# Retention of 1024 tokens in two halves: pairs of tokens within a half, a split sum of keys by decayed values for the other half

## The chip, the cores and the metric

The kernel runs on one core of a Trainium2 chip. The metric is the time of one execution on the device in microseconds (us); lower is better. The core has five engines that run side by side, each in the order of its own list of instructions: TensorE (PE in the profile, its weight loads PEld), VectorE (DVE), ScalarE (ACT), GpSimd (POOL) and SyncE (SP). SP issues nearly all transfers here, one after the other, so a transfer that waits holds back those that stand behind it.

## What is computed

One encoder layer for two sequences, a sample of 1024 tokens and a prompt of 512. The change touches one part of it, the retention mixer, which works on four heads of 128 features. The reference goes through each sequence in chunks of 128 tokens with a running state, once forward and once backward. Cut to what matters:

```
q = rotary(heads(u[..., :D_RET]))
k = rotary(heads(u[..., D_RET:2 * D_RET])) * (RET_HEAD_DIM ** -0.5)
v = heads(u[..., 2 * D_RET:3 * D_RET])
...
s = einsum('bhncd,bhnjd->bhncj', qc, kc) * Dm        # pairs within a chunk, decayed
intra = einsum('bhncj,bhnje->bhnce', s, vc)
...
Rn = R * gC + einsum('bhcd,bhce->bhde', kk, vv)      # state: keys by decayed values
cross = einsum('bhncd,nbhde->bhnce', qc * wq, states)
return (intra + cross).reshape(B, H, L, d)
...
o = o_f + o_b
o = o * lax.rsqrt(mean(o * o, axis=-1, keepdims=True) + NORM_EPS)
return jax.nn.silu(g) * o
```

Written out, the output of token c is the sum over all tokens j of (q_c . k_j) times decay(|c - j|) times v_j, with one decay rate forward and one backward. The decay is an exponential, so for tokens j that all lie on one side of c it splits into a factor of c and a factor of j.

## The kernel before

All matrix products are made from 32-bit operands split into a high and a low part (`hi_act`, line 59, on ACT makes the high part; `lo`, line 62, the low one), and `mm3` (lines 67 to 69) adds three products of them in PSUM.

The part in question is the third stage of the layer's middle. On PE it holds two kinds of work, interleaved. The main work projects the prompt's 512 tokens with `w_in` (tile `wips`, 24 blocks of 24 products each; function `w_in_pass`) and makes their values (tile `v`, 96 products; function `w_in_v`). Beside it runs `retention`, first for the sample (four heads of 1024 tokens), then for the prompt (512 tokens). `gen_run(main, side, per)` writes both into the program: after each step of the main work, `per` steps of the side work. The build then orders each engine's list with a scheduler that goes by its own estimate of times, so what stands where on an engine is not the written order.

`retention` for one head of 1024 tokens loads q, k and v of all tokens (tile `qkraw`, `vraw`) and splits them (`qkh`, `qkl`, `vh`, `vl`; the low parts on POOL). Then, for each half of 512 tokens and each of the eight blocks of 128 keys: three products give the scores (`st`), DVE multiplies them with the decay (`sm`, line 999), ACT and DVE split the result (`sh`, `sl`), and three products add it to the output (`o`). These are 16 such pairs for a head, 6 products of 512 columns each. The decay of a head (`mask`, function `decay`) is a table over the distance of two tokens, 1920 columns wide. Behind each half comes a tail that normalises it: two products (`ss`), a row of ACT (`row`), and then, through SP and POOL in turn, `cmp`, `rs`, `rr` and `y`.

The program goes on with `load_mats` (tile `mraw`, then `mh` and `ml`: matrices that the next stage needs) and `filter_spectra` (tile `ftap`, transposed into `tr` on PE, then `fw`). The matrices are loaded into the memory of the activations that the projections read, so they can't start before the last `wips` product.

The stage ahead of it (function `mix_in_consts`, `ret_consts`, then `w_in_pass` for the sample beside the filter's own work `filter_taps`, tile `tapps`) starts with loads of constants, among them `delta`, the distances for `decay`.

Of the kernel before, what the change touches and what calls it, by code (L numbers as in the profile page):

```python
# [8 lines left out]
F32 = mybir.dt.float32  # L9
# [37 lines left out]
class Kern:  # L47
# [885 lines left out]

    def ret_consts(self, p):
        nc = self.nc
        self.delta = p.tile([128, 1920], F32, name="delta", bufs=1)
        nc.sync.dma_start(self.delta, self.io["delta"])
        self.lg = p.tile([128, 2, 4], F32, name="lg", bufs=1)
        for i, n in enumerate(("lgf", "lgb")):
            nc.sync.dma_start(self.lg[:, i], self.io[n].broadcast_to([128, 4]))  # L940
        self.nlb = p.tile([128, 4], F32, name="nlb", bufs=1)
        nc.vector.tensor_scalar(self.nlb, self.lg[:, 1], -1.0, None, ALU.mult)
        self.lscale = p.tile([128, 1], F32, name="lscale", bufs=1)
        nc.gpsimd.memset(self.lscale, float(np.log(128.0 ** -0.5)))

    def decay(self, p, h, a, b):


        nc = self.nc
        arg = p.tile([128, 1920], F32, tag="mask", name="mask", bufs=2)  # L950
        lf, lb, nlb = self.lg[:, 0, h:h + 1], self.lg[:, 1, h:h + 1], self.nlb[:, h:h + 1]
        c = slice(896, 1024)
# [4 lines left out]
        nc.scalar.activation(arg[:, a:896], self.delta[:, a:896], AF.Exp, bias=self.lscale, scale=nlb)  # L957
        nc.scalar.activation(arg[:, c], arg[:, c], AF.Exp, bias=self.lscale)
        nc.scalar.activation(arg[:, 1024:b], self.delta[:, 1024:b], AF.Exp, bias=self.lscale, scale=lf)
        return arg  # L960

    def retention(self, L, base, h, d, p, pss, pso):
        nc = self.nc
        nj = L // 128
        cols = slice(base, base + L)
        arg = self.decay(p, h, 896 - (L - 128), 896 + L)
        hn = 1024 // L
        if h % hn == 0:
            qk = []
            for i in range(2):  # L970
                raw = p.tile([128, hn, L], F32, tag="qkraw", name="qkraw", bufs=2)
                for j in range(hn):
                    nc.sync.dma_start(raw[:, j], d["qk"][4 * i + h + j][:, cols])
                hi = p.tile([128, hn, L], F32R, tag=f"qkh{i}", name="qkh", bufs=2)
                lo = p.tile([128, hn, L], F32R, tag=f"qkl{i}", name="qkl", bufs=2)
                self.hi_act(hi, raw)
                self.lo(nc.gpsimd, lo, raw, hi)
                qk += [hi, lo]
            raw = p.tile([128, nj, hn * 128], F32, tag="qkraw", name="vraw", bufs=2)
            for j in range(nj):  # L980
                nc.sync.dma_start(raw[:, j], d["v"][base // 128 + j][:, h * 128:(h + hn) * 128])
            hi = p.tile([128, nj, hn * 128], F32R, tag="vh", name="vh", bufs=2)
            lo = p.tile([128, nj, hn * 128], F32R, tag="vl", name="vl", bufs=2)
            self.hi_act(hi, raw)
            self.lo(nc.gpsimd, lo, raw, hi)
            self.qkv = qk + [hi, lo]
        qh, ql, kh, kl = (t[:, h % hn] for t in self.qkv[:4])
        vh, vl = (t[:, :, h % hn * 128:h % hn * 128 + 128] for t in self.qkv[4:])
        yield
        for c0 in range(0, L, 512):  # L990
            cc = slice(c0, c0 + 512)
            o = pso.tile([128, 512], F32, tag="o", name="o")
            for j in range(nj):
                s = pss.tile([128, 512], F32, tag="st", name="st")
                jj = slice(j * 128, j * 128 + 128)
                self.mm3(s, kh[:, jj], kl[:, jj], qh[:, cc], ql[:, cc], True, True)
                x = c0 - 128 * j + 896
                sm = p.tile([128, 512], F32, tag="sm", name="sm", bufs=4)
                nc.vector.tensor_tensor(sm, s, arg[:, x:x + 512], ALU.mult)
                sh = p.tile([128, 512], F32R, tag="sh", name="sh", bufs=4)  # L1000
                sl = p.tile([128, 512], F32R, tag="sl", name="sl", bufs=4)
                self.hi_act(sh, sm)
                self.lo(nc.vector, sl, sm, sh)
                self.mm3(o, vh[:, j], vl[:, j], sh, sl, j == 0, j == nj - 1)
                if j % 2:
                    yield
            sq = p.tile([128, 512], F32, tag="sq", name="sq", bufs=1)
            nc.scalar.activation(sq, o, AF.Square)
            sh = p.tile([128, 512], F32R, tag="sqh", name="sqh", bufs=1)
            sl = p.tile([128, 512], F32R, tag="sql", name="sql", bufs=1)  # L1010
# [41 lines left out]
    def build(self, xs, outs):  # L1052
# [22 lines left out]
        with ExitStack() as right:  # L1075
# [10 lines left out]
            with pool("raw", 2) as raw, pool("w", 4) as wp, pool("scw") as gp, pool("rope") as rop:  # L1086
                self.mix_in_consts(gp, rop)
                self.ret_consts(rop)
                with pool("g", 4) as gp, pool("nrm") as self.np, pool("xin", 2) as self.xp, pool("hT2") as hp2, pool("wi", 2, space=PSUM) as psw, \
# [122 lines left out]
def dft_consts():  # L1212
# [10 lines left out]
    for L in (1024,512):  # L1223
# [7 lines left out]
    c['delta']=(np.arange(1920)[None]-896-np.arange(128)[:,None]).astype(np.float32)  # L1231
    return c


# [15 lines left out]
```

## Time and profile before

| | before |
|---|---|
| median of 3 runs | 3393.17 us (3390.63 to 3396.44) |
| profiled execution: time, span of the profile | 3399.09 us, 3397.3 us |
| PE busy, share of the span | 3087.7 us, 91% |
| DVE busy | 2644.2 us, 78% |
| ACT busy | 1431.3 us, 42% |
| POOL busy | 555.3 us, 16% |
| first `st` product, last `y` of the retention's tails | 1493.6 us, 1786.0 us |
| last `wips` product of the stage | 1800.2 us |

Busy time is the time in which an engine had an instruction at work; for a PE that is fed without a gap it is 100% of a stretch. The times of the trace count from the start of the span.

### The profile page before, as it was taken

The page shows a single profiled execution, that of the slowest core. Times are in us where ns is not written, and L with a number is a line of the kernel's source. Part 1 is how long each engine was busy: PE and PEld are TensorE (multiplying, and loading weights), DVE is VectorE, ACT ScalarE, POOL GpSimd, SP SyncE. Part 2 cuts the span into 40 slices and gives each one's busy share as a digit, 9 for nine tenths or more (in the row PEclk, how much of TensorE's full clock was granted, in tenths as well). Part 3 has the DMA queues.
Part 4 walks back from the last instruction along what each step waited for, and adds up shares of the span by engine and source line. Part 5 has one row for each costly group of instructions (what it writes and reads, how often), then busy time and mean ns, then how long its engine had stood idle before and what let it go on. Part 6 is the DMA issues. An engine that isn't in the chain of part 4 may idle for free. (4 is left out here: it accounts for less than half of the span.)

```text
span 3397.3 us, 46267 instructions
## 1 busy us (share of the span) xinstructions
PE 3087.7 (91%) x16792; PEld 2885.7 (85%) x16792; DVE 2644.2 (78%) x4316; ACT 1431.3 (42%) x2373; POOL 555.3 (16%) x400
## 2 busy tenths in 40 slices
PE   5999998999897799989897998984899999999996
PEld 4999998999897677767676887763899999999996
DVE  8788788777877599678655878886888788877776
ACT  4333464333444234355543344332433455333453
POOL 0000000000200323365322544552000000000000
PEclk8999999999998899999998999997999999999998
DMA  3567454322344534453453125454377544422343
GB/s 128 211 232 286 123 156 143 84 72 75 103 131 139 169 117 160 150 172 112 120 173 128 44 83 172 153 172 139 127 266 272 190 147 134 143 72 72 87 128 131
DMA packets 218806, 485.34 MB, mean 143 GB/s; under 512 B 36432, under 2 KB 64464, under 8 KB 216400
## 3 DMA queue, kind: packets, MB, share of 16 engines
q1 hardware_dynamic: 218576, 482.37, 43.3%
q8 instruction: 132, 2.16, 0.3%
q14 instruction: 98, 0.80, 0.1%
HBM read 382.60 MB, written 99.65 MB: 142 GB/s over the span
## 5 line engine op out<-in xcount | busy, mean ns | idle before, releaser
L68 PE MATMUL dn<-xl,w2h 128*128 128x384 f32 x1232 | 414.8, 337 | 12.7 <-DVE xl L62 12.7
L59 ACT ACTIVATE wh<-raw 128x512 fp32r<-128x512 f32 (+1 forms) x312 | 216.6, 694 | 446.0 <-PE ua L68 96.4
L59 ACT ACTIVATE wh<-s 128x512 fp32r<-128x512 f32 x352 | 221.7, 631 | 427.7 <-PE ua L68 122.3
L69 PE MATMUL dn<-xh,w2l 128*128 128x384 f32 x1232 | 392.4, 337 | 0.0
L67 PE MATMUL dn<-xh,w2h 128*128 128x384 f32 x1232 | 386.8, 337 | 1.7 <-ACT xh L59 1.6
L59 ACT ACTIVATE w2h<-raw 128x512 fp32r<-128x512 f32 (+1 forms) x348 | 236.6, 682 | 342.4 <-PE dn L68 214.9
L62 DVE TENSOR_TENSOR wl<-s,wh 128x512 fp32r<-128x512 f32 x352 | 241.8, 688 | 168.5 <-PE ub L68 84.2
L95 POOL TENSOR_TENSOR r<-m,mhalf 128x3 f32<-128x3 f32 (+1 forms) x35 | 38.8, 1108 | 1847.8 <-DVE m L94 1846.9
L62 DVE TENSOR_TENSOR w2l<-raw,w2h 128x512 fp32r<-128x512 f32 (+1 forms) x316 | 219.5, 705 | 126.0 <-ACT w2h L59 107.7
L67 PE MATMUL wips<-hh,wh 128*128 128x512 f32 x576 | 231.9, 403 | 17.7 <-ACT wh L59 16.7
L68 PEld LDWEIGHTS dn<-xl,w2h 128*128 128x128 f32 x1232 | 232.5, 189 | 15.3 <-DVE xl L62 15.3
L67 PEld LDWEIGHTS dn<-xh,w2h 128*128 128x128 f32 x1232 | 229.5, 189 | 3.8 <-ACT xh L59 3.3
L69 PE MATMUL wips<-hh,wl 128*128 128x512 f32 x576 | 230.7, 401 | 1.8 <-POOL wl L62 1.2
L68 PE MATMUL wips<-hl,wh 128*128 128x512 f32 x576 | 230.8, 401 | 0.0
L69 PEld LDWEIGHTS dn<-xh,w2l 128*128 128x128 f32 x1232 | 230.5, 189 | 0.0
L62 DVE TENSOR_TENSOR wl<-raw,wh 128x512 fp32r<-128x512 f32 (+1 forms) x276 | 199.0, 721 | 39.9 <-ACT wh L59 37.9
L67 PE MATMUL fw<-th,mh 128*128 128x256 f32 x448 | 132.3, 297 | 30.9 <-DVE spec L839 18.2
L67 PEld LDWEIGHTS wips<-hh,wh 128*128 128x128 f32 x576 | 110.4, 192 | 46.3 <-ACT wh L59 17.6
L67 PE MATMUL ua<-b11h,wh 128*128 128x384 f32 x352 | 123.7, 351 | 26.6 <-ACT b11h L59 26.6
L69 PEld LDWEIGHTS wips<-hh,wl 128*128 128x128 f32 x576 | 110.3, 192 | 30.0 <-POOL wl L62 2.4
L68 PE MATMUL fw<-tl,mh 128*128 128x256 f32 x448 | 132.3, 296 | 1.3 <-DVE tl L62 1.2
L69 PE MATMUL fw<-th,ml 128*128 128x256 f32 x448 | 130.1, 291 | 3.8 <-POOL ml L62 3.0
(342 smaller groups left out, 9088.9 us busy)
## 6 DMA issues: line engine op xcount, KB each, us to landing
raw<-ffn_w SPq DMA_DIRECT2D x440, 256.0 KB, 2.7
raw<-ws SPq DMA_DIRECT2D x220, 256.0 KB, 2.6
wsum<-ffn_w SPq DMA_DIRECT2D x60, 768.0 KB, 7.5
raw<-w_in_f SPq DMA_DIRECT2D x48, 512.0 KB, 4.3
ws<-wsum SPq DMA_DIRECT2D x30, 768.0 KB, 4.2
xq<-x SPq DMA_DIRECT2D x16, 768.0 KB, 7.2
res<-x SPq DMA_DIRECT2D x16, 768.0 KB, 6.3
raw<-w_out SPq DMA_DIRECT2D x24, 512.0 KB, 3.4
```

The lines of the kernel that those rows point to most:

```text
L59: self.nc.scalar.activation(hi, src, AF.Copy)
L62: eng.tensor_tensor(lo, src, hi.bitcast(F32), ALU.subtract)
L67: mm(ps, lhsT=ah, rhs=bh, start=first, stop=False, **kw)
L68: mm(ps, lhsT=ah, rhs=bl, start=False, stop=False, **kw)
L69: mm(ps, lhsT=al, rhs=bh, start=False, stop=last, **kw)
L95: nc.gpsimd.tensor_tensor(r, m, self.mhalf[:, :n], ALU.pow)
```

## The change

For the sample, `retention` now goes through the pairs of tokens of one half only: 8 pairs of 512 tokens with 128 keys for a head in place of 16. What the other half adds to a half's output comes from a new function, `half_state`. It transposes k of the other half on PE (`kt`, four of 128 columns) and splits it (`kth`, `ktl`), multiplies v with its part of the decay (`vs`, four of ACT) and splits it (`vsh`, `vsl`), and sums keys by values over the four blocks (`rs`, 12 products of 128 columns). The sum is split (`rsh`, `rsl`), q is multiplied with its part of the decay (`qw`) and split (`qsh`, `qsl`), and three products add the result to `o` (line L67 to L69, `o<-qsh,rsh` and so on) ahead of the pairs. For a head this happens twice, once for each half. The decay's table shrinks from 1920 columns to 896. `ret_consts` loads a table of distances (`dist`) and one of positions (`kdist`), and ACT makes the factors of the keys (`kw`, 8 small exponentials) there. Buffers change: three for `qkraw` and `vraw` in place of two, three for `sm`, `sh` and `sl` in place of four, shared with the tail. Two steps of the side work follow each step of the main work in place of four. The prompt's retention (512 tokens, one half) keeps its pairs.

The diff, without what only repeats:

```
     def ret_consts(self, p):
         nc = self.nc
-        self.delta = p.tile([128, 1920], F32, name="delta", bufs=1)
+        self.delta = p.tile([128, 896], F32, name="delta", bufs=1)
         nc.sync.dma_start(self.delta, self.io["delta"])
+        self.dist = p.tile([128, 2, 512], F32, name="dist", bufs=1)
+        nc.sync.dma_start(self.dist, self.io["dist"].broadcast_to([128, 2, 512]))
+        kd = p.tile([128, 2, 4], F32, name="kdist", bufs=1)
+        nc.sync.dma_start(kd, self.io["kdist"])
...
+        self.kw = p.tile([128, 2, 4, 4], F32, name="kw", bufs=1)
+        for i in range(2):
+            for h in range(4):
+                nc.scalar.activation(self.kw[:, i, h], kd[:, i], AF.Exp, bias=self.lscale, scale=self.lg[:, i, h:h + 1])
...
+    def half_state(self, i, h, p, pss, q, k, v):
+        nc = self.nc
+        ps = pss.tile([128, 512], F32, tag="st", name="kt")
+        for t in range(4):
+            nc.tensor.transpose(ps[:, t * 128:t * 128 + 128], k[:, t * 128:t * 128 + 128], self.ident)
+        kh = p.tile([128, 4, 128], F32R, tag="kth", name="kth", bufs=1)
+        kl = p.tile([128, 4, 128], F32R, tag="ktl", name="ktl", bufs=1)
+        ps = ps.rearrange("p (t c) -> p t c", c=128)
+        self.hi_act(kh, ps)
+        self.lo(nc.vector, kl, ps, kh)
+        w = p.tile([128, 4, 128], F32, tag="vs", name="vs", bufs=1)
+        for t in range(4):
+            nc.scalar.activation(w[:, t], v[:, t], AF.Copy, scale=self.kw[:, i, h, t:t + 1])
...
+        self.hi_act(vh, w)
+        self.lo(nc.vector, vl, w, vh)
+        ps = pss.tile([128, 512], F32, tag="st", name="rs")[:, :128]
+        for t in range(4):
+            self.mm3(ps, kh[:, t], kl[:, t], vh[:, t], vl[:, t], t == 0, t == 3)
...
+        self.hi_act(rh, ps)
+        self.lo(nc.vector, rl, ps, rh)
+        w = p.tile([128, 512], F32, tag="qw", name="qw", bufs=1)
+        nc.scalar.activation(w, self.dist[:, i], AF.Exp, scale=self.lg[:, i, h:h + 1])
+        nc.vector.tensor_tensor(w, w, q, ALU.mult)
...
+        self.hi_act(qh, w)
+        self.lo(nc.vector, ql, w, qh)
+        return rh, rl, qh, ql
 
     def retention(self, L, base, h, d, p, pss, pso):
...
-                raw = p.tile([128, hn, L], F32, tag="qkraw", name="qkraw", bufs=2)
+                raw = p.tile([128, hn, L], F32, tag="qkraw", name="qkraw", bufs=3)
...
+            if nj > 4:
+                q, k = (r[:, 0] for r in raws)
+                self.far = [self.half_state(i, h, p, pss, q[:, 512 - 512 * i:1024 - 512 * i], k[:, 512 * i:512 * i + 512],
+                                            raw[:, 4 * i:4 * i + 4]) for i in (1, 0)]
...
-            for j in range(nj):
+            if nj > 4:
+                rh, rl, sh, sl = self.far[c0 // 512]
+                self.mm3(o, rh, rl, sh, sl, True, False)
+            for j in range(c0 // 128, c0 // 128 + 4):
...
-                sm = p.tile([128, 512], F32, tag="sm", name="sm", bufs=4)
+                sm = p.tile([128, 512], F32, tag="sm", name="sm", bufs=3)
...
-                    gen_run(main(), side(1024, 0), 4)
+                    gen_run(main(), side(1024, 0), 2)
```

How it moves instructions, at three places. The first is on SP, at the start of the stage ahead, where the projections' first weights (`raw<-w_in_f`) are loaded behind the activations `x`; `row` is a small store that waits for DVE. One piece of the difference:

```order
 L166 DMA x<-x_001_74 128x2x256
+L422 DMA row_89<-r 128x3x1
 L166 DMA x<-x_100_77 128x2x256
-L698 DMA raw<-w_in_f 128x1024
-L422 DMA row_89<-r 128x3x1
-L698 DMA raw<-w_in_f 128x1024
+L698 DMA raw<-w_in_f 128x1024 x2
```

The small store now stands ahead of the first load of weights, not behind it.

The second is on PE, at the first head of the retention. Before, the first scores stand between blocks of the projection:

```order
L69 MATMUL wips<-hh,wl 128x512
L67 MATMUL st<-qkh 128x512 x3
L67 MATMUL wips<-hh,wh 128x512
L68 MATMUL wips<-hl,wh 128x512
L69 MATMUL wips<-hh,wl 128x512
```

With the change the sum of keys by values of the second half stands there, with the transposes for the first half in its middle:

```order
L68 MATMUL wips<-hl,wh 128x512
L67 MATMUL rs<-vsh,kth 128x128
L976 MATMUL kt<-ident,qkraw 128x128 x4
L68 MATMUL rs<-vsl,kth 128x128
L69 MATMUL rs<-vsh,ktl 128x128
L67 MATMUL rs<-vsh,kth 128x128
```

PE now meets, two products into a block of the projection, one that waits for `vsh` and `kth` of ACT and then for `vsl` and `ktl` of DVE, and the rest of that block stands behind it.

The third is on SP, at the end of the stage. `hy` are stores of the projections, `cmp`, `rs`, `rr` and `y` belong to a tail of the retention. Before:

```order
L1022 DMA cmp<-row 128x1x4
L714 DMA hy_96<-o 128x512
L828 DMA ftap<-tap_00_147 128x2048
L828 DMA ftap<-tap_01_148 128x2048
L823 DMA turn<-turn 128x24
L698 DMA raw<-w_in_f 128x1024
L1025 DMA rs_146<-r 128x4
L714 DMA hy_97<-o 128x512
L698 DMA raw<-w_in_f 128x1024
L1027 DMA rr<-rs_146 128x512
```

With the change:

```order
L776 DMA mraw<-mats 128x1024 x2
L823 DMA turn<-turn 128x48
L1073 DMA cmp<-row 128x1x4
L828 DMA ftap<-tap_00_147 128x2048
L714 DMA hy_102<-o 128x512
L828 DMA ftap<-tap_01_148 128x2048
L823 DMA turn<-turn 128x24
L776 DMA mraw<-mats 128x1024 x2
L1076 DMA rs_146<-r 128x4
L1078 DMA rr<-rs_146 128x512
L776 DMA mraw<-mats 128x640 x3
L1081 DMA y_134<-yr 128x512
```

The last tail and the two loads `ftap` now stand among the loads of the matrices, at the very end of the stage; before, they stood ahead of the projections' last loads of weights.

## Rows read from the trace of the kernel before

**Rows 1.** Page, part 1: busy time, share of the span, instructions
```profile
PE 3087.7 (91%) x16792; PEld 2885.7 (85%) x16792; DVE 2644.2 (78%) x4316; ACT 1431.3 (42%) x2373; POOL 555.3 (16%) x400
```

**Rows 2.** Each stretch: length, then PE, PEld, DVE, ACT, POOL busy; clock; DMA; GB/s
```profile
1136.75:1478.86 342.11, 327.93 (x1363) 259.73 (x1364) 283.01 (x468) 134.31 (x209) 113.52 (x50) 0.97 0.41 145
1478.86:1800.20 321.34, 290.86 (x1203) 227.33 (x1202) 220.23 (x289) 162.72 (x233) 134.46 (x122) 0.96 0.45 142
1478.86:1520.00 41.14, 37.76 (x150) 29.40 (x149) 29.10 (x38) 24.54 (x31) 31.11 (x15) 0.92 0.60 194
1520.00:1660.00 140.00, 129.47 (x545) 100.54 (x544) 117.09 (x154) 81.22 (x123) 69.61 (x62) 1.00 0.39 115
1660.00:1720.00 60.00, 48.31 (x185) 37.05 (x185) 29.22 (x36) 27.32 (x36) 19.01 (x18) 0.91 0.55 175
1720.00:1760.00 40.00, 39.98 (x173) 32.05 (x172) 27.59 (x41) 18.54 (x30) 9.04 (x17) 1.00 0.39 113
1760.00:1800.20 40.20, 35.34 (x157) 28.29 (x156) 17.22 (x23) 11.11 (x16) 5.69 (x12) 0.92 0.47 165
1800.20:1840.00 39.80, 22.67 (x119) 19.36 (x117) 15.32 (x28) 13.64 (x23) 16.58 (x14) 0.66 0.54 185
1840.00:1880.00 40.00, 38.97 (x306) 37.45 (x307) 32.52 (x58) 16.90 (x32) 10.38 (x8) 1.00 0.14 54
```

**Rows 3.** Waits of PE, 1478.86 to 1800.2: total, times, longest
```profile
PE v L67 <- ACT w2h L59: 8.9, 2, 5.5
PE o L68 <- DVE sl L62: 5.6, 6, 3.0
PE tr L795 <- DMA ftap<-tap: 4.9, 2, 2.6
PE st L67 <- ACT qkh L59: 3.0, 1, 3.0
```

**Rows 4.** Groups by line, 1478.86 to 1800.2: busy, mean ns, idle before
```profile
L62 DVE TENSOR_TENSOR sl<-sm,sh 128x512 fp32r<-128x512 f32 x80 | 76.5, 973 | 16.0 <-ACT sh L59 15.6
L999 DVE TENSOR_TENSOR sm<-st,mask 128x512 f32<-128x512 f32 x80 | 53.3, 681 | 7.2 <-PE st L69 7.2
L59 ACT ACTIVATE sh<-sm 128x512 fp32r<-128x512 f32 x80 | 48.8, 626 | 67.4 <-DVE sm L999 62.8 <-PE o L69 3.9 <-PE st L69 0.6
```

**Rows 5.** PE in order of time around eight transposes: start, duration
```profile
1793.60 1.03 PE L795 MATMUL tr<-ident,ftap 128*128 128x128 f32 x8
1794.39 0.48 PE L67 MATMUL wips<-hh,wh 128*128 128x512 f32 x1
```

**Rows 6.** ACT on the decay's table: duration ns min/median/max
```profile
L957 ACT ACTIVATE mask<-delta,lscale,nlb x8: 707/914/1137, 1481.2 to 1685.2; 128x896 f32<-128x896 f32 x4, 128x384 f32<-128x384 f32 x4
L958 ACT ACTIVATE mask<-mask,lscale x8: 381/394/404, 1486.4 to 1686.9; 128x128 f32<-128x128 f32 x8
```

**Rows 7.** Start of the stage ahead, in order of time: SP, ACT, PE
```profile
1122.05 0.67 SPq L698 DMA_DIRECT2D raw<-w_in_f  x1
1123.66 0.36 SPq L422 DMA_DIRECT2D row<-r  x1
...
1135.64 1.06 ACT L59 ACTIVATE wh<-raw 128x1024 fp32r<-128x1024 f32 x1 [5.80 <-DMA raw<-w_in_f]
...
1136.75 0.79 PE L67 MATMUL wips<-hh,wh 128*128 128x512 f32 x1 [16.01 <-ACT wh L59]
```

**Rows 8.** Waits of SP's queue, 1478.86 to 1800.2: total, times, longest
```profile
SPq L1025 <- POOL r L100: 51.7, 12, 11.7
SPq L1030 <- POOL yr L1029: 47.5, 12, 5.5
```

**Rows 9.** SP in order of time around the end of the stage
```profile
1770.87 0.87 SPq L828 DMA_DIRECT2D ftap<-tap  x2
...
1800.26 0.81 SPq L776 DMA_DIRECT2D mraw<-mats  x2
```

More of the change, by code (lines that the diff above doesn't have):

```diff
@@ L944, in ret_consts, with decay @@
         nc.gpsimd.memset(self.lscale, float(np.log(128.0 ** -0.5)))
-    def decay(self, p, h, a, b):
+        self.kw = p.tile([128, 2, 4, 4], F32, name="kw", bufs=1)
+        for i in range(2):
+            for h in range(4):
+                nc.scalar.activation(self.kw[:, i, h], kd[:, i], AF.Exp, bias=self.lscale, scale=self.lg[:, i, h:h + 1])
+    def decay(self, p, h):
         nc = self.nc
-        arg = p.tile([128, 1920], F32, tag="mask", name="mask", bufs=2)
+        arg = p.tile([128, 896], F32, tag="mask", name="mask", bufs=2)
         lf, lb, nlb = self.lg[:, 0, h:h + 1], self.lg[:, 1, h:h + 1], self.nlb[:, h:h + 1]
-        c = slice(896, 1024)
+        a, c, b = slice(0, 384), slice(384, 512), slice(512, 896)
         m2 = p.tile([128, 128], F32, tag="m2", name="m2", bufs=1)
@@ L956, in decay @@
         nc.vector.tensor_tensor(arg[:, c], m2, arg[:, c], ALU.subtract)
-        nc.scalar.activation(arg[:, a:896], self.delta[:, a:896], AF.Exp, bias=self.lscale, scale=nlb)
+        nc.scalar.activation(arg[:, a], self.delta[:, a], AF.Exp, bias=self.lscale, scale=nlb)
         nc.scalar.activation(arg[:, c], arg[:, c], AF.Exp, bias=self.lscale)
-        nc.scalar.activation(arg[:, 1024:b], self.delta[:, 1024:b], AF.Exp, bias=self.lscale, scale=lf)
+        nc.scalar.activation(arg[:, b], self.delta[:, b], AF.Exp, bias=self.lscale, scale=lf)
         return arg
+    def half_state(self, i, h, p, pss, q, k, v):
[11 more added lines that the diff above has]
+            nc.scalar.activation(w[:, t], v[:, t], AF.Copy, scale=self.kw[:, i, h, t:t + 1])
+        vh = p.tile([128, 4, 128], F32R, tag="vsh", name="vsh", bufs=1)
+        vl = p.tile([128, 4, 128], F32R, tag="vsl", name="vsl", bufs=1)
+        self.hi_act(vh, w)
[3 more added lines that the diff above has]
+            self.mm3(ps, kh[:, t], kl[:, t], vh[:, t], vl[:, t], t == 0, t == 3)
+        rh = p.tile([128, 128], F32R, tag="rsh", name="rsh", bufs=2)
+        rl = p.tile([128, 128], F32R, tag="rsl", name="rsl", bufs=2)
+        self.hi_act(rh, ps)
[3 more added lines that the diff above has]
+        nc.vector.tensor_tensor(w, w, q, ALU.mult)
+        qh = p.tile([128, 512], F32R, tag="qsh", name="qsh", bufs=2)
+        ql = p.tile([128, 512], F32R, tag="qsl", name="qsl", bufs=2)
+        self.hi_act(qh, w)
+        self.lo(nc.vector, ql, w, qh)
+        return rh, rl, qh, ql
     def retention(self, L, base, h, d, p, pss, pso):
@@ L965, in retention @@
         cols = slice(base, base + L)
-        arg = self.decay(p, h, 896 - (L - 128), 896 + L)
+        arg = self.decay(p, h)
         hn = 1024 // L
         if h % hn == 0:
-            qk = []
+            qk, raws = [], []
             for i in range(2):
-                raw = p.tile([128, hn, L], F32, tag="qkraw", name="qkraw", bufs=2)
+                raw = p.tile([128, hn, L], F32, tag="qkraw", name="qkraw", bufs=3)
+                raws.append(raw)
                 for j in range(hn):
@@ L978, in retention @@
                 qk += [hi, lo]
-            raw = p.tile([128, nj, hn * 128], F32, tag="qkraw", name="vraw", bufs=2)
+            raw = p.tile([128, nj, hn * 128], F32, tag="qkraw", name="vraw", bufs=3)
             for j in range(nj):
@@ L996, in retention @@
                 self.mm3(s, kh[:, jj], kl[:, jj], qh[:, cc], ql[:, cc], True, True)
-                x = c0 - 128 * j + 896
-                sm = p.tile([128, 512], F32, tag="sm", name="sm", bufs=4)
+                x = c0 - 128 * j + 384
+                sm = p.tile([128, 512], F32, tag="sm", name="sm", bufs=3)
                 nc.vector.tensor_tensor(sm, s, arg[:, x:x + 512], ALU.mult)
-                sh = p.tile([128, 512], F32R, tag="sh", name="sh", bufs=4)
-                sl = p.tile([128, 512], F32R, tag="sl", name="sl", bufs=4)
+                sh = p.tile([128, 512], F32R, tag="sh", name="sh", bufs=3)
+                sl = p.tile([128, 512], F32R, tag="sl", name="sl", bufs=3)
                 self.hi_act(sh, sm)
                 self.lo(nc.vector, sl, sm, sh)
-                self.mm3(o, vh[:, j], vl[:, j], sh, sl, j == 0, j == nj - 1)
+                self.mm3(o, vh[:, j], vl[:, j], sh, sl, nj == 4 and j == 0, j % 4 == 3)
                 if j % 2:
                     yield
-            sq = p.tile([128, 512], F32, tag="sq", name="sq", bufs=1)
+            sq = p.tile([128, 512], F32, tag="sm", name="sq", bufs=3)
             nc.scalar.activation(sq, o, AF.Square)
-            sh = p.tile([128, 512], F32R, tag="sqh", name="sqh", bufs=1)
-            sl = p.tile([128, 512], F32R, tag="sql", name="sql", bufs=1)
+            sh = p.tile([128, 512], F32R, tag="sh", name="sqh", bufs=3)
+            sl = p.tile([128, 512], F32R, tag="sl", name="sql", bufs=3)
             self.hi_act(sh, sq)
@@ L1230, in dft_consts @@
         c[f'turn{L}']=np.ascontiguousarray(t.reshape(-1,128,6).transpose(1,0,2)).astype(np.float32)
-    c['delta']=(np.arange(1920)[None]-896-np.arange(128)[:,None]).astype(np.float32)
+    c['delta']=(np.arange(896)[None]-384-np.arange(128)[:,None]).astype(np.float32)
+    c['dist']=np.stack([np.arange(512),511-np.arange(512)])[None].astype(np.float32)
+    pos=np.arange(128)[:,None]+128*np.arange(4)[None]
+    c['kdist']=np.stack([512-pos,1+pos],1).astype(np.float32)
     return c
```

## The prediction

> **What bounds the kernel now.** I read the page first: PE is busy for 91% of the span [rows 1], so work taken from PE is worth time wherever PE is fed. Then I cut the trace into stretches [rows 2]. The retention lies between 1478.86, the first projection of its stage, and 1800.20, the last one. The reader is to see three things there. PE is busy for 291 of 321 us, DVE for 220, ACT for 163: PE is the bound, though in the densest part (1520 to 1660) DVE has 117 of 140 us and isn't far behind. From 1720 to 1760 pairs of the prompt's retention and projections are mixed without any gap: 173 products in 39.98 us, 0.231 us for one product of 512 columns. With that price the stage has a lower bound: 1176 products of 512 columns (576 `wips`, 96 `v`, 400 for the sample's retention, 104 for the prompt's) take 271.7 us, the 27 others recorded in it, transposes priced below, 2.7. The remaining 47 us of the 321 are lost. By stretch, each length less its count by 0.231 (the transposes of the last one by 0.10): 6.5 us up to 1520, 14 up to 1660, 17 up to 1720, none up to 1760, 7 up to 1800. The waits of PE tell where [rows 3]: 8.9 us on weights of `v`, 5.6 on the low part of decayed scores, 4.9 on the load `ftap`, 3.0 on the first k; the rest is short, or time at the lower clock behind a gap (granted 0.92 and 0.91 in the stretches with gaps). After 1800.20 comes a poor stretch: 23 of 40 us busy at a granted 0.66, while the matrices are loaded.
>
> **What the change takes from and gives to PE.** A head loses 8 of 16 pairs, 48 products of 512 columns. It gains 6 such products (the far part of two halves), 24 of 128 columns (`rs`) and 8 transposes (`kt`). Over four heads that is 168 products fewer at 0.231, or -38.8 us. Eight transposes of 128 columns take from 1793.60 to the next product's start at 1794.39 [rows 5], 0.10 us each; so 32 of them cost 3.2 us. A product of 128 columns with two split operands isn't in the trace. Below it lies the transpose, 0.10, above it the mixture of 1840 to 1880, mostly products of 256 columns: 306 in 38.97 us, 0.127 [rows 2]. I take 0.11, nearer the transpose since its width is the same: 96 cost 10.6 us, 9.6 to 12.2 by the bounds. The sum on PE is **-25.0 us** (-26 to -22.5).
>
> The Trainium skill, TensorE: Matmul & The Clock Gate, section Back-to-back issue gap, states some 81 ns for a product of 128 columns in a stream with its weight loads, and 131 for one of 512. The second doesn't agree with the 0.231 us of this trace. By the first figure the 96 products would cost 7.8 us and the sum would be -27.8; by the ratio of the two, which speaks against cutting work into narrow products, they would cost 13.7 and the sum would be -21.9.
>
> **What it does to the other engines.** ACT loses 8 `sh` of 626 ns a head [rows 4] and about 0.86 us of decay (two tables of 896 columns become two of 384, 1.137 to 0.707 us [rows 6]). Twice it gains three splits of 512 columns (0.63 each), four `vs` and one `rsh` of 128 columns (0.39 each [rows 6]) and one exponential of 512 (0.7 to 0.9, between the widths of the same rows): 4.6 us a half. That is +3.3 us a head, 13 in all: 176 of some 300 us. DVE loses 8 `sm` and 8 `sl` a head, 13.2 us by their means [rows 4], and gains twice four operations of 512 columns at about 0.7 and one of 128 at 0.3 (an estimate, between a quarter and a half of the wide one), 6.2 us: -28 us in all. Neither becomes the bound, and these sums cost the end nothing: PE's work covers them. Without that cover ACT's 13 us would count. ACT also gets three more loads of a function table and eight small exponentials in the stretch before (1136.75 to 1478.86), where it's busy for 134 of 342 us; they are costed at nothing for the same reason, and at most they are a few us.
>
> **Waits that come, go and move, in the stage.** At the start PE waits 3.0 us for the split k. Now it needs k only as loaded (a little earlier), but then meets the first `rs`. Behind its load stand on ACT `kth`, four `vs` and `vsh`, and on DVE `ktl` and `vsl`; ACT's list has the split of the next head's q, which waits for a transfer, ahead of `vsh`. What is late next is everything behind `rs` on PE, 22 products of a projection. I price that at +5 us, from 0 (the projections cover it) to 10 (the chain of some 6 us, and the lower clock behind it). In the middle half of the pairs' waits go, and eight `rs` and `o<-qsh` come that can wait in the same way; I put this at 0, from -6 to +6. The weights of `v` are loaded between the tails on SP, and the tails are as many as before; but `v` is now mixed with pairs of the third and fourth head, which fill PE meanwhile: -5 of 17, from -12 to 0. The wait of 4.9 us on `ftap` leaves the stage: -4, from -7 to -2. The sum is **-4 us**, from -25 to +14.
>
> **What moves past the stage's end.** Before, `ftap` was issued 29 us ahead of the first matrix [rows 9], and its transposes ran between projections. Now both loads (1 MB each) stand behind the first two matrices, and the last tail's `rs`, `rr` and `y` stand ahead of matrices too. In exchange the loads `z` and `gate` of the next step, which stood among the matrices, come later, with much the same bytes. PE has 17 idle us in that stretch [rows 2]. I take **+4 us**; below is -1, since the transposes leave the full stretch; above is +11, 2 MB at the 185 GB/s of that stretch.
>
> **The start of the stage ahead.** The projections' first weights were issued at 1122.05, ahead of the small store at 1123.66 [rows 7]; now they stand behind it and behind two more issues of SP, which take 0.36 to 0.67 us in the same rows. ACT waited for them until 1135.64 and PE until 1136.75, 16 us. The bytes of the constants don't change (960 KB become 448 and 512). All of a delay is on the path: +1.5 us, from 0 to 2.5.
>
> The sum is -25.0 - 4 + 4 + 1.5 = -23.5 us, on the profiled execution's 3399.09 (1.8 outside its span of 3397.3), and the median of the runs stands 5.9 below that execution. From the median: **3370 us**, 0.7% faster. With all ends on one side it would be -53 or +5.
>
> **The rivals.**
> *The gain is eaten by the chains of the half states.* Eight times PE meets an `rs` that waits for ACT and DVE in their order. If each costs 3 us, the length of PE's wait for the first split k, 24 us are gone and the time is 3393. For it: ACT is the engine with the longest lists of waits for transfers, and its load rises. Against it: the scheduler has put 20 and more products between the transposes and the sums of later heads, and in 1720 to 1760 the mixture left no gap.
>
> *Slower, through SP at the stage's end.* `rs` waits for POOL 4.3 us on average, 11.7 at most, and `y` up to 5.5 [rows 8]. If the last tail holds the matrices for 11.7 and 5.5 us, and `ftap` comes 11 later, that is 28 us on the path, with 2.5 at the start and the sums' 5: 36 against 25 and the 4 of `ftap` that leaves. The time would be about 3400. It decides from some 29 us of delay on. Against it: the matrices go through two buffers, and SP waited for their splits anyway.
>
> *A larger gain.* If the lost 47 us shrink in proportion to the pairs, as the evenly mixed stretch without a gap suggests, another 20 us go: 3350. Against it: the losses on `v`, the start and the matrices have nothing to do with pairs.
>
> **How the numbers follow.** My forecast, a gain of 9 to 40 us, gets 0.66; the larger gain 0.07; the eaten gain 0.15; slower 0.12. About 0.2% (6.8 us) is what a measurement of this kernel can tell from no change. So faster 0.73, the same 0.15, slower 0.12. The forecast's own range is 3353 to 3384. The range that should hold the time is 3353 to 3398: it leaves out the larger gain and the slower case and takes in the eaten gain, which the bounds allow.
>
> **What would show it.** In the profile of the changed kernel: 168 fewer wide products, 96 `rs` at 0.10 to 0.127 us in a row; the first `rs` waiting for ACT or DVE for about 5 us; the stage from its first to its last `wips` shorter by about 29 us; DVE's busy time lower by 20 to 28 us, ACT's higher by some 17; the first `wips` of the stage ahead later by 1.5; the stretch behind the last `wips` longer by some 4. I would be wrong if PE's waits on `rs`, `kth` or `vsl` sum to over 15 us, if the matrices come later by more than 11, or if stages that the change doesn't touch are ordered in a worse way.

## The result and the profile after

| | before | after |
|---|---|---|
| median of the runs (4 each) | 3394.79 us (3390.63 to 3396.44) | 3355.22 us (3354.42 to 3355.58) |
| span of the profiled execution | 3397.3 us | 3352.6 us |
| first `wips` of the retention's stage | 1478.86 us | 1473.70 us |
| start of the stage's last product (`wips` or `ss`) | 1799.8 us | 1756.1 us |

The ratio is 0.9885, with a 95% interval of 0.9868 to 0.9902: 39.6 us faster by the medians, where the forecast was 23.5. Of the 44.7 us between the two profiled spans, 38.5 lie in the stage (320.9 us before, 282.4 after, from its first to its last product). Ahead of the stage lie 5.2, behind it 1.0.

The page's first part after the change, which answers to [rows 1]:

```profile
PE 3056.8 (91%) x16752; PEld 2869.0 (86%) x16752; DVE 2624.0 (78%) x4292; ACT 1445.8 (43%) x2424; POOL 555.1 (17%) x400
```

PE has 31 us less, DVE 20 less, ACT 14.5 more. The stretches of the changed kernel, with the columns of [rows 2]:

```profile
1473.70:1755.60 281.90, 263.07 (x1134) 211.84 (x1133) 205.10 (x259) 166.62 (x266) 134.82 (x115) 0.94 0.50 151
1473.70:1515.00 41.30, 31.22 (x118) 24.65 (x117) 32.40 (x35) 25.09 (x41) 28.63 (x13) 0.79 0.62 204
...
1700.00:1755.60 55.60, 55.60 (x241) 45.05 (x240) 37.56 (x54) 25.41 (x39) 15.04 (x27) 1.00 0.42 114
1755.60:1795.40 39.80, 22.05 (x145) 19.39 (x144) 23.38 (x34) 16.21 (x28) 19.44 (x21) 0.83 0.75 265
```

The first 41 us of the stage have become poorer: PE busy for 31.22 us at a granted 0.79, where it was 37.76 at 0.92 [rows 2]. The last 55.6 us of the stage have no gap. Behind the stage PE is busy for 22 of 40 us as before, though the transfers run at 265 GB/s in place of 185.

PE's waits in the changed stage, which answer to [rows 3]:

```profile
PE rs L68 <- DVE vsl L62: 5.3, 1, 5.3
PE ss L1065 <- ACT sqh L59: 2.9, 1, 2.9
PE o L68 <- DVE sl L62: 2.7, 2, 1.5
PE wips L67 <- DVE o L719: 2.3, 1, 2.3
PE kt L976 <- DMA qkraw<-qk: 2.2, 1, 2.2
...
PE rs L69 <- DVE ktl L62: 1.1, 1, 1.1
```

The 8.9 us on the weights of `v` and the 4.9 on `ftap` have left the stage; 5.3 us on `vsl` have come.

For the experiments I use one more quantity, the **lost time** of a stage: its length as in the table, less its work on PE by the prices of the prediction (a wide product 0.231 us, `rs` 0.11, a transpose 0.10). Before: 320.9 - 271.7 - 2.7 = 47 us. After: 282.4 less 1008 wide products (232.8), 10.6 and 3.2, so 36 us. The change saved 25 us of work, 2.7 of transposes that now lie behind the stage, and 11 of lost time, where I had put 4. Each lost time is read from one profiled execution, and such executions differ by several us: the changed kernel and the one of the second experiment below, whose lists for PE are the same, took 1596.5 and 1603.2 us from the stage's last product to the end. A few us between two lost times are no finding by themselves; where it matters, the medians of the runs stand beside them.

### The profile page after: what moved, and what is told of

The parts are those of the page before. It is cut to its first block, busy times and chain, and to the rows that moved or that the text cites. A ratio compares the mean times of both kernels' runs of the same rounds, so it can differ in the third digit from the quotient of the medians.

```text
span 3352.6 us, 46218 instructions
## 1 busy us (share of the span) xinstructions
PE 3056.8 (91%) x16752; PEld 2869.0 (86%) x16752; DVE 2624.0 (78%) x4292; ACT 1445.8 (43%) x2424; POOL 555.1 (17%) x400
## 5 line engine op out<-in xcount | busy, mean ns | idle before, releaser
L69 PE MATMUL dn<-xh,w2l 128*128 128x384 f32 x1232 | 392.2, 336 | 0.0
L67 PE MATMUL dn<-xh,w2h 128*128 128x384 f32 x1232 | 387.3, 337 | 3.2 <-ACT xh L59 3.2
L67 PE MATMUL wips<-hh,wh 128*128 128x512 f32 x576 | 232.9, 405 | 18.2 <-DVE vo L750 14.4
L67 PEld LDWEIGHTS dn<-xh,w2h 128*128 128x128 f32 x1232 | 229.5, 189 | 5.2 <-ACT xh L59 4.8
L69 PE MATMUL wips<-hh,wl 128*128 128x512 f32 x576 | 231.8, 403 | 1.2 <-POOL wl L62 1.2
L69 PEld LDWEIGHTS dn<-xh,w2l 128*128 128x128 f32 x1232 | 230.0, 188 | 0.0
L67 PE MATMUL fw<-th,mh 128*128 128x256 f32 x448 | 131.9, 296 | 25.9 <-DVE spec L839 22.5
L67 PEld LDWEIGHTS wips<-hh,wh 128*128 128x128 f32 x576 | 111.0, 193 | 46.4 <-ACT wh L59 14.8
L67 PE MATMUL ua<-b11h,wh 128*128 128x384 f32 x352 | 123.8, 352 | 26.4 <-ACT b11h L59 26.4
L69 PEld LDWEIGHTS wips<-hh,wl 128*128 128x128 f32 x576 | 111.1, 193 | 28.8 <-POOL wl L62 1.9
L68 PEld LDWEIGHTS wips<-hl,wh 128*128 128x128 f32 x576 | 111.3, 193 | 26.4
```

The lines of the kernel that those rows point to most:

```text
L67: mm(ps, lhsT=ah, rhs=bh, start=first, stop=False, **kw)
L68: mm(ps, lhsT=ah, rhs=bl, start=False, stop=False, **kw)
L69: mm(ps, lhsT=al, rhs=bh, start=False, stop=last, **kw)
```

## The experiments

Where did 11 us of lost time go? The first theory was the interleave (two steps for four), its rivals were the buffers, and that half the pairs simply bring half the waits.

**The interleave alone, on the kernel before.**

```
-                    gen_run(main(), side(1024, 0), 4)
+                    gen_run(main(), side(1024, 0), 2)
```

> The kernel before with two steps of the side work after each step of the main work in place of four; nothing else. The changed kernel lost 11.7 us less in its stage than its smaller work on PE explains. Theory A, the interleave did that: the values v are now mixed with pairs here too, the wait of 8.9 us on their weights goes, and the time falls by 5 to 12 us against the kernel before, to about 3383 to 3390. Theory B, it came with there being fewer pairs (fewer places where PE waits): no change here, within 5 us of the kernel before.

Measured: 3384.86 us against 3397.75 for the kernel before in the same comparison, ratio 0.9968 (0.9957 to 0.9980). Lost time 33 us, and no wait on the weights of `v` is left. So in the kernel before the interleave is worth 13 us by the medians (11 by the ratio), about what theory A said.

**The interleave undone in the changed kernel** is the other half of that test (the same line, with 4 for 2).

> The changed kernel with four steps of the side work after each step of the main work, as in the kernel before; nothing else. The lists of PE and POOL come out the same as with two, the others nearly so. Theory: this part of the change is worth nothing here, within 4 us of 3355. Rival: the moved loads on SP (v of the third head ahead of a tail's load) cost or give more than 5 us.

Measured: 3354.48 us, ratio 0.9877 (0.9863 to 0.9890) to before, lost time 34 us: no difference from the changed kernel. The build makes the same list for PE from both. So what the interleave gives alone, it doesn't give on top of the rest of the change.

**All buffers of the change, on the kernel before.** Sixteen pairs a head, no half states.

```
-                raw = p.tile([128, hn, L], F32, tag="qkraw", name="qkraw", bufs=2)
+                raw = p.tile([128, hn, L], F32, tag="qkraw", name="qkraw", bufs=3)
...
-                sm = p.tile([128, 512], F32, tag="sm", name="sm", bufs=4)
+                sm = p.tile([128, 512], F32, tag="sm", name="sm", bufs=3)
...
-            sq = p.tile([128, 512], F32, tag="sq", name="sq", bufs=1)
+            sq = p.tile([128, 512], F32, tag="sm", name="sq", bufs=3)
```

> The kernel before with the buffers of the changed one: three for the loaded q, k and v in place of two, three for the scores' tiles in place of four, shared with the tail. Theory A2, the third buffer lets the next head's loads start earlier and did the 11.7 us: 5 to 12 us faster than the kernel before. Theory B, it came with there being fewer pairs: within 5 us, or some us slower for the fewer score tiles.

Measured: 3364.96 us against 3397.75, ratio 0.9905 (0.9892 to 0.9919): **33 us faster with all of the old work**, nearly three times the most that either theory gave. The stage of this kernel, as stretch and as waits of PE:

```profile
1470.70:1757.00 286.30, 277.27 (x1178) 220.66 (x1176) 217.92 (x285) 157.05 (x225) 123.28 (x110) 0.99 0.48 153
```
```profile
PE o L68 <- DVE sl L62: 3.9, 4, 1.4
PE st L67 <- ACT qkh L59: 3.0, 1, 3.0
PE ss L1014 <- ACT sqh L59: 1.4, 1, 1.4
```

PE is busy for 277 of 286 us at a granted 0.99; lost time is 14 us. To see what the buffers did, I counted the products `st` in each stretch. Columns: length, PE's busy time in them (count), clock, DMA share, GB/s. First the kernel before:

```profile
1520.00:1560.00 40.00, 13.71 (x46) 1.00 0.42 128
1560.00:1600.00 40.00, 15.72 (x54) 1.00 0.43 130
...
1680.00:1720.00 40.00, 2.40 (x9) 0.91 0.64 207
...
1760.00:1800.20 40.20, 0.00 (x0) 0.92 0.47 165
```

And with the new buffers:

```profile
1510.00:1550.00 40.00, 8.48 (x30) 1.00 0.46 145
1550.00:1590.00 40.00, 11.73 (x44) 1.00 0.39 118
...
1630.00:1670.00 40.00, 11.41 (x42) 1.00 0.53 166
1670.00:1710.00 40.00, 10.08 (x36) 1.00 0.32 116
1710.00:1756.90 46.90, 7.37 (x27) 1.00 0.40 113
```

Before, the scores stand densely in the first two thirds, so that DVE is busy for 37.85 of 40 us in the first of these stretches and PE waits for `sl`. They are nearly used up when the products of `v` come: 9 in the stretch from 1680, where PE waits for weights. With the new buffers the build lays them out over the whole stage; `v` lies among them, and a late weight costs nothing.

**Which buffers? The third for the loaded q, k and v alone.**

> The kernel before with three buffers for the loaded q, k and v in place of two; nothing else. All buffers of the change together made the kernel before 33 us faster, with an almost full PE in the stage. Theory A2, it's the third buffer (the loads and splits of a head no longer wait for each other, so the heads come earlier and the pairs reach into v and the last projections): 25 us or more of the 33, to about 3362 to 3372. Theory A3, it's the tail, which no longer shares single buffers of its own: at most 8 us here.

Measured: 3382.51 us against 3395.65, ratio 0.9965 (0.9951 to 0.9978), 13 us. The layout stays uneven (54 `st` in the 40 us from 1553.4, 12 in the 40 from 1673.4), but the loads come earlier (the sample's last `vraw` starts 75 us behind the stage's first `wips`, where it was 107), and of the waits for weights of `v` this is left, with 1.3 us for their low part:

```profile
PE v L67 <- ACT w2h L59: 1.6, 1, 1.6
```

**The score tiles alone**, three shared with the tail for four and a set of its own.

> The kernel before with three score tiles each in place of four, shared with the tail of a half, which had one of its own of each; nothing else. Theory A2 (the third buffer for q, k and v): within 5 us of the kernel before. Theory A3 (the tail's buffers): 20 us or more faster, to about 3375 or below.

Measured: 3373.30 us against 3395.65, ratio 0.9934 (0.9921 to 0.9946), 22 us, with lost time 17. A3's number held here and failed in the run above, so neither theory stands alone: both buffers count, and the two parts, 13 and 22, make up the 33. That fewer tiles for the scores gain time is against what one expects of buffers; the even layout appears here too (34, 42, 36, 42 and 36 `st` in the five stretches of 40 us from 1516).

**What the far part costs: left out.**

```
-                self.far = [self.half_state(i, h, p, pss, q[:, 512 - 512 * i:1024 - 512 * i], k[:, 512 * i:512 * i + 512],
-                                            raw[:, 4 * i:4 * i + 4]) for i in (1, 0)]
...
-                rh, rl, sh, sl = self.far[c0 // 512]
-                self.mm3(o, rh, rl, sh, sl, True, False)
```

> The changed kernel without the other half: no half_state and no product of it, so a half's output is the sum over its own 512 tokens alone. PE has 96 rs products (0.11 us each), 32 transposes (0.10) and 24 products of 512 columns (0.231) less, 19.3 us. Theory 1, the far part costs its PE work and nothing else: 3336 us. Theory 2, its chains cost as well (the first rs waited 5.3 us and a stretch at a granted clock of 0.79 lies around it): 25 to 32 us less, 3323 to 3330. Rival, much of it fills gaps of PE: less than 12 us less, above 3343.

Measured: 3334.77 us (3328.15 to 3340.87), 20.5 below the changed kernel: theory 1, the work on PE. But lost time is still 29 us, against 14 with the same buffers and all sixteen pairs. So **halving the pairs brings back 15 us of lost time** (the interleave, which was worth nothing on the changed kernel, and the decay's table differ between these two kernels as well). The medians say much the same: 30.2 us faster than the kernel with the same buffers, for 44.4 us of work, so 14 are given back. The largest hole in this kernel, on SP, ACT and PE in order of time, then DVE and POOL beside it:

```profile
1585.85 0.51 SPq L1066 DMA_DIRECT2D cmp<-row  x1
1594.26 0.32 SPq L1069 DMA_DIRECT2D rs<-r  x1
1594.68 0.37 SPq L737 DMA_DIRECT2D raw<-w_in_v  x1
```
```profile
1599.55 1.06 ACT L59 ACTIVATE w2h<-raw 128x1024 fp32r<-128x1024 f32 x1 [7.61 <-DMA raw<-w_in_v]
```
```profile
1603.07 0.79 PE L67 MATMUL o<-sh,vh 128*128 128x512 f32 x1 [3.37 <-ACT sh L59]
1608.00 0.80 PE L68 MATMUL o<-sl,vh 128*128 128x512 f32 x1 [4.14 <-DVE sl L62]
```
```profile
1602.80 2.37 DVE L963 TENSOR_SCALAR mask<-delta,lg 128x128 f32<-128x128 f32 x1
1605.09 2.85 DVE L62 TENSOR_TENSOR sl<-sm,sh 128x512 fp32r<-128x512 f32 x1
```
```profile
1601.75 5.64 POOL L62 TENSOR_TENSOR qkl<-qkraw,qkh 128x1024 fp32r<-128x1024 f32 x2
```

The store `rs` of a tail waits on SP until 1594.26, a load of `v`'s weights stands behind it, ACT waits 7.61 us for that load, the split `sh` of a pair stands behind it on ACT, and PE waits 3.37 us for it. The 4.14 us behind that have another cause: `sh` is there, but DVE is late with `sl`. An operation of the decay's table takes 2.37 us ahead of it, where the shortest of its eight took 0.27, and `sl` itself 2.85, both while POOL splits q and k (the last section comes back to that). For the first of the two waits, as many tails and loads stand in the queues as with sixteen pairs, and PE has 44 us less work (192 products) to cover them.

**The far part made twice** (the second time unused).

```
-                                            raw[:, 4 * i:4 * i + 4]) for i in (1, 0)]
+                                            raw[:, 4 * i:4 * i + 4]) for i in (1, 0) for _ in range(2)][1::2]
```

> The changed kernel with each half_state made twice, the first result unused: 96 more rs products and 32 more transposes on PE, 13.8 us by their prices, and 13 us more each for ACT and DVE. Theory 1, the cost is PE's work: 3369 us, 12 to 16 us more. Theory 2, the chains through ACT and DVE cost too: 25 us more or above, with waits on kth, vsh or vsl that sum to over 15 us.

Measured: 3386.60 us, 31 above the changed kernel for 13.8 of work, with lost time 53. Theory 2's size came, but not its waits: `rs` waited 4.2 us for `vsl` and nothing else of the half states appears among the larger waits; 9.9 us were for `sl`, the pairs' own. That ACT and DVE, with more to do, come later to the pairs would fit, but no run took that apart.

**Can the start be mended?** The changed kernel's start lost 16 us up to 1515 (41.3 less 98 wide products, 12 `rs` and 8 transposes) against 6.5 before. PE there, in order of time:

```profile
1499.02 0.33 PE L67 MATMUL rs<-vsh,kth 128*128 128x128 f32 x1 [0.19 <-ACT vsh L59]
1499.19 0.62 PE L976 MATMUL kt<-ident,qkraw 128*128 128x128 f32 x4
1505.14 0.47 PE L68 MATMUL rs<-vsl,kth 128*128 128x128 f32 x1 [5.33 <-DVE vsl L62]
...
1507.55 0.73 PE L69 MATMUL wips<-hh,wl 128*128 128x512 f32 x1
1508.08 0.63 PE L67 MATMUL wips<-hh,wh 128*128 128x512 f32 x1
```

Three edits tried to mend it: the far part added behind the pairs of a half, with its half state written after the first two pairs; each half state written right ahead of its own half; and, with that, two score tiles in place of three. One more took the two score tiles alone. None did: the first 40 us of the stage lost 15.7 to 16.6 us in all four, where the changed kernel lost 16.9.

```
-                self.mm3(o, rh, rl, sh, sl, True, False)
...
+                if nj > 4 and j % 4 == 1:
+                    i = 1 - c0 // 512
+                    q, k, v = self.raws
+                    far = self.half_state(i, h, p, pss, q[:, cc], k[:, 512 * i:512 * i + 512], v[:, 4 * i:4 * i + 4])
+                if nj > 4 and j % 4 == 3:
+                    rh, rl, sh, sl = far
+                    self.mm3(o, rh, rl, sh, sl, False, True)
```

> The changed kernel with the far part added to o behind the pairs of a half in place of ahead of them, and half_state written behind the first two pairs; the same work. Theory: the change pays some 20 us of new lost time for the chains of the half states, most of it up to 1515 us, where PE meets the first rs before DVE has its operands (5.3 us and a granted clock of 0.79); with pairs to do first, 5 to 12 us come back: 3343 to 3350. Rival: the chain is moved, not shortened, and the raw q, k and v are held longer, which delays the next head: 3355 or slower.

Measured: 3362.72 us, 7.5 slower than the changed kernel: the rival. PE waits 4.4 us for `vsl` all the same, and 12.4 for the tails (`ss`).

```
+            if nj > 4:
+                i = 1 - c0 // 512
+                q, k, v = self.raws
+                rh, rl, sh, sl = self.half_state(i, h, p, pss, q[:, cc], k[:, 512 * i:512 * i + 512], v[:, 4 * i:4 * i + 4])
```

> The changed kernel with the half_state of each half written right ahead of that half's pairs, not both at the start of the head; the same work. The first head then meets one chain of kt, vs and rs at the start, with two scores in its middle, not two. Theory C (what the chains of the half states cost lies at the start of a head): 5 to 10 us faster than the changed kernel, 3345 to 3350. Theory S (evenness): the pairs now end 117 rows ahead of the last projection, where they ended 67 ahead: no gain, 3355 to 3362, as when the far part was added last.

Measured: 3363.36 us. Theory C fell; the time is 1.4 us above the range of theory S.

```
-                sm = p.tile([128, 512], F32, tag="sm", name="sm", bufs=3)
+                sm = p.tile([128, 512], F32, tag="sm", name="sm", bufs=2)
```

The same holds for `sh`, `sl` and the tail.

> The changed kernel with two score tiles each (sm, sh, sl, shared with the tail) in place of three. In PE's list the pairs now reach to the last projection and behind it, where they ended 67 rows ahead of it. Theory S (lost time goes by how evenly the pairs lie between the projections and the products of v, and fewer tiles make the build lay them out more evenly): 5 to 12 us faster than the changed kernel, 3343 to 3350. Rival: two tiles are too few, PE waits for sh and sl of the pair before: over 15 us of such waits and 3360 or above.

> Both edits together: half_state ahead of its half's pairs, and two score tiles in place of three. In PE's list no piece of 60 rows up to the last projection holds fewer than 8 or more than 23 products of pairs, but for those of v (6 to 32). Theory S: the most even list, so the least lost time, 12 us or more below the changed kernel, 3343 or less. Theory C: no faster than with the half states alone moved. Rival of both: waits on sh and sl, 3360 or above.

Measured: 3363.90 us with two score tiles alone, 3371.82 with both edits. Theory S fell too: the most even list was the slowest of the four, with 9.8 us of waits on `sh` and `sl`. With two score tiles alone the rival's time came without its waits (4.1 us on `sh` and `sl`, where it wanted over 15; the largest was 5.7 on `rsh`). Evenness went with less lost time in the kernel with sixteen pairs; in the changed kernel it is not what is missing, so that it was the cause there isn't shown either.

**The first head without its far part**, on the same lines as the far part left out, with `if nj > 4 and h:`.

> The changed kernel with the other half left out for the first head alone (its outputs are the sums over their own 512 tokens); the other three heads keep their half states. PE has a quarter of the far part less, 4.8 us by its prices. Theory 1, the first head's chains cost nothing beyond their work on PE, since leaving out all four heads' far parts gave just their PE work (20 us): about 3350. Theory 2, the chain at the start of the stage, where PE waits 5.3 us for the first rs and runs at a granted clock of 0.79, is dear and the others are covered: 12 to 18 us less, 3337 to 3343, with the stretch from the first projection to 40 us behind it holding 15 to 25 more products of 512 columns' worth of work.

Measured: 3348.17 us, 7 below the changed kernel for 4.8 of work: nearer to theory 1. The start stays poor: 114 products of 512 columns in its first 40 us, at a granted 0.83, lose 13.7 us, where the changed kernel lost 16.9 in its own. That is some 14 such products more, just under the 15 to 25 of theory 2, whose time didn't come. PE now waits for DVE in another place, and DVE's list shows why:

```profile
1497.77 2.82 DVE L62 TENSOR_TENSOR qsl<-qw,qsh 128x512 fp32r<-128x512 f32 x1
1500.52 1.87 DVE L1050 TENSOR_TENSOR sm<-st,mask 128x512 f32<-128x512 f32 x3
```
```profile
1501.25 0.80 PE L67 MATMUL st<-qkh 128*128 128x512 f32 x1 [3.89 <-DVE sm L1050]
```

The second head's `qsl` stands ahead of the first head's `sm`, and takes 2.82 us. The test didn't take the half states' work from the start, as theory 2 needed; it only let the next head's come there.

## Why the prediction was right, and where it was off

Direction and main term were right; the size of the waits was not.

**PE's work, -25.0 us.** Confirmed. At full clock the `rs` products stand 0.11 us apart, as I chose:

```profile
1517.73 0.27 PE L67 MATMUL rs<-vsh,kth 128*128 128x128 f32 x1
1517.84 0.27 PE L68 MATMUL rs<-vsl,kth 128*128 128x128 f32 x1
```

Leaving the far part out gave 20.5 us where these prices give 19.3. An estimate by the figures of the Trainium skill, TensorE: Matmul & The Clock Gate, section Back-to-back issue gap, would be 16.5 with the first (0.081 for 0.11) and 22.4 with their ratio; the pace of these rows agrees with neither. Two slips in the working change nothing: with all ends on one side it is -52 and not -53, and the upper bound of -22.5 holds only with the transposes at 0.127 too; at the 0.10 that stands there it is -23.4.

**The other engines.** ACT rose by 14.5 us over the span, where I gave some 17, but in the stage only from 162.7 to 166.6, where I gave 176 (3.6 us of it are splits that went behind the stage with their transposes; the rest isn't worked out). DVE fell by 20 over the span and by 15 in the stage, not 28: I priced the half states' operations at 0.7 us, and three of the four take more.

```profile
L998 DVE TENSOR_TENSOR qw<-qw,qkraw 128x512 f32<-128x512 f32 x8 | 11.0, 1381 | 8.8 <-ACT qw L997 7.9 <-DMA qkraw<-qk 0.9
...
L62 DVE TENSOR_TENSOR qsl<-qw,qsh 128x512 fp32r<-128x512 f32 x8 | 9.7, 1215 | 6.5 <-ACT qsh L59 6.5
L62 DVE TENSOR_TENSOR vsl<-vs,vsh 128x512 fp32r<-128x512 f32 x8 | 9.4, 1172 | 1.0 <-ACT vsh L59 1.0
...
L62 DVE TENSOR_TENSOR ktl<-kt,kth 128x512 fp32r<-128x512 f32 x8 | 5.5, 683 | 0.8 <-ACT kth L59 0.8
```

These four give 35.6 us in place of 22.4, which is the difference. I had costed them at nothing on the end, since PE covers them; at the start it doesn't.

**Waits in the stage, -4 us: the step that was mis-sized.** It measured -11, and that is the sum of large terms of which I had none. The sum had no term at all for the buffers, though the diff shows them. On the kernel before they alone take lost time from 47 to 14 us. Halving the pairs raises it to 29, and the half states to 36: +22 in all, which my terms for the start (+5) and the middle (0) had at 5. The medians, which hang on no single trace, give the same order with a smaller sum: 3397.75 to 3364.96 by the buffers (-32.8); to 3334.77 with half the pairs gone (-30.2, with 14 of the work's 44 given back); to 3355.22 with the half states (+20.5 for 19.3 of work, so 1 given back and not 7: the profiled run without the far part was the fastest of its five, 6.6 us below their median). So the gain lies in the forecast's range in part by luck: a term of -33 and one of +15 to +22, each larger than the whole sum of the waits, were left out, and they cancel for the greater part. The start alone cost 10, the upper end of its range. The wait on `v` went as forecast, with its whole 8.9 us, but for a reason that I had only half: on the kernel before it went with the new buffers alone, which spread the pairs, and with the interleave alone, so it didn't need fewer pairs. One limit stays: the buffers were taken apart on the kernel before only; the changed kernel with the old ones was not run, so how its 11 us divide is an inference from kernels that differ by one step each.

**Behind the stage, +4 us.** It measured -1.0 (1597.5 us from the last product's start to the end before, 1596.5 after), which is less than the 6.7 us between the two traces with the same list for PE. Nearer by, `a`, the first product of the next stage, came 59.3 us behind the last product before and 57.1 after: no sign of the +4. The order on SP came as forecast:

```profile
1756.18 0.90 SPq L776 DMA_DIRECT2D mraw<-mats  x2
...
1758.15 0.59 SPq L828 DMA_DIRECT2D ftap<-tap  x1
...
1759.26 0.43 SPq L828 DMA_DIRECT2D ftap<-tap  x1
```

and PE waits for it there, where it waited for the matrices before:

```profile
PE tr L795 <- DMA ftap<-tap: 11.8, 2, 9.3
```

Both loads seem to have found room in one stretch, whose transfers run at 265 GB/s in place of 185; no run took that apart.

**The start of the stage ahead, +1.5 us.** This can't be told: the first `wips` came at 1133.0 in place of 1136.75, but kernels that keep the old code there had it anywhere from 1130.1 to 1134.9.

**The rivals.** *The larger gain* came nearest in number (3350 for 3355.2) and its reason is refuted: lost time does not shrink with the pairs, it doubles from 14 to 29 when 32 of the 80 go. *The eaten gain* is seen in part: PE's waits for `vsl`, `ktl` and `vsh` sum to 6.6 us, far from 24, but against the kernel with the same buffers and all pairs the change gains only 7 to 10 us of its 25 (39.6 against 32.8 to the kernel before, or 3355.22 against 3364.96). *Slower, through SP*, has its mechanism in the kernel without the far part, in the middle of the stage, and not at its end.

## What to carry to other kernels

Where a build orders the lists by its own estimates, the number of tiles in a diff is a change of order: price it, even where no instruction is added. How evenly the side work lies beside the main work is one thing to look at, but it wasn't enough to tell: it went with a gain on the kernel before and with losses on the changed one. Test the small parts of a change on the kernel before; there the buffers alone gave 33 us, where the whole change gave 40. Work that is removed from the engine that bounds a stage was also the cover of its queues, so expect part of the saving back as waits: here some 15 of 44 us when half of the sample's pairs were left out with nothing in their place.

## What the runs showed of the hardware

**DVE beside POOL.** At the start of the stage `vsl` took 2.82 us, where its shortest of eight took 0.68. DVE, then POOL, of the changed kernel in order of time:

```profile
1494.35 0.68 DVE L62 TENSOR_TENSOR ktl<-kt,kth 128x512 fp32r<-128x512 f32 x1
...
1499.51 2.83 DVE L721 TENSOR_TENSOR o<-o,sw 128x512 f32<-128x512 f32 x1
1502.27 2.82 DVE L62 TENSOR_TENSOR vsl<-vs,vsh 128x512 fp32r<-128x512 f32 x1
1505.01 0.68 DVE L719 TENSOR_TENSOR o<-wips,rope 128x512 f32<-128x512 f32 x1
```
```profile
1499.00 2.79 POOL L62 TENSOR_TENSOR vl<-vraw,vh 128x1024 fp32r<-128x1024 f32 x1
1501.76 2.78 POOL L62 TENSOR_TENSOR qkl<-qkraw,qkh 128x1024 fp32r<-128x1024 f32 x1
```

The two slow operations of DVE have both inputs in SBUF, and each ends some 0.55 us behind a split of POOL that began before it, about the time that it takes alone. `ktl` ahead of them and the `o` behind them read one input from PSUM and take 0.68, though POOL is at work too. The Trainium skill, SBUF — State Buffer, section SBUF: two separate sides, states that DVE with two inputs in SBUF and a GpSimd operation that reads SBUF hold one pair of ports in turn, each for its whole instruction; these rows agree. The slow `mask` in the kernel without the far part (2.37 us) reads but one tensor from SBUF and a scalar, so two inputs are not the only case that was slow beside POOL. It is a part of why PE's first `rs` was late, and of the largest hole without the far part. It may be why moving the half states about did not help, since POOL's splits of q, k and v lie at the same place; no run moved these splits.

**The clock behind a wait.** Behind the wait of 5.33 us the `rs` stand 0.21 us apart and the wide products 0.43, twice their price, up to 1512. That piece was granted 0.50, the lower level of 1.2 GHz:

```profile
1505.10:1512.00 6.90, 6.86 (x22) 5.89 (x23) 5.81 (x5) 3.52 (x8) 6.29 (x3) 0.50 0.66 229
```

From 1512.3 to 1520 the clock is granted in full and the products stand at their price again. For the 11 `rs` and 11 wide products of that piece this makes some 3.4 us (1.1 and 2.3) on top of the wait.
